# Output products of the recurrent groups, emitted some steps of attention behind the casts of their operands

## The chip, the cores and the metric

The kernel runs on one core of one Trainium2 chip. What is measured is the time of one execution in device microseconds; of several runs the median counts. TensorE is called PE here, its weight loads PEld, VectorE DVE, ScalarE ACT, GpSimd POOL, and the engine that issues the loads from memory SP.

## The reference, cut to what matters

The reference is a trunk of two layers over 256 context tokens and 512 latent tokens of width 1024. In each layer one input projection is split into three groups: A is latent attention with 4 heads, B a bidirectional mLSTM, C a bidirectional RG-LRU. Their outputs are put side by side and go through one output projection.

```python
def token_mixing(ul, uc, ...):
    al, ml_, rl = jnp.split(ul @ w_in, split_at, axis=-1)
    ...
    ya_l, ya_c = mla_mixer(al, ac, rope, g_q, w_uq, g_kv, w_ukv, with_ctx_out)
    yb_l, yb_c = mlstm_mixer(ml_, mc, ml_gate_bias, with_ctx_out)
    yc_l, yc_c = rglru_mixer(rl, rc, conv_w, conv_b, w_a, b_a, w_x, b_x, lam, with_ctx_out)
    y_l = jnp.concatenate([ya_l, yb_l, yc_l], axis=-1) @ w_out
...
        xl = xl + g1l * yl
        xl = xl + g2l * squared_relu_mlp(modulate(rms_norm(xl), sh2l, sc2l), w_ff1[l], w_ff2[l])
```

The last layer needs no output for the context tokens, so there most work is on the 512 latent tokens alone.

## The kernel before, in words

Everything is held transposed: features on the 128 partitions, tokens along the free dimension. A float32 operand is split into a rounded part and a rest (names ending in h and l, or whi and wlo for weights), and a product is three matmuls: h by whi, l by whi, h by wlo. ACT makes the rounded part by a cast, DVE the rest by a subtraction (`split_raw` at lines 165 to 169 for weights, `split_act` at lines 177 and 178 for activations). `dense` (line 196) runs such products over the chunks of the contraction, and yields a cost behind each chunk; one chunk on one range of tokens is called a step here, three matmuls.

The output projection is cut in two. `out_proj` multiplies the half of w_out that belongs to attention once attention is done. `ybc` multiplies the other half, for groups B and C, beside attention: it splits the four chunks of their outputs (tiles yBCh and yBCl), and then, for four pieces of w_out, splits the weights and runs two chunks of output, for each range of tokens four steps into a PSUM tile `outp`, which `gated_add` (line 426, on DVE) adds to x. Layer 0 works on both ranges of tokens (256 and 512 wide, 64 steps in all), layer 1 on the latent one (32 steps).

Two lists of work are written as generators and woven by `weave`: it always advances the one whose sum of yielded costs is the smaller. One is the input projection of attention, its queries and `attention`; the other is mlstm and then `ybc`, whose costs are scaled by PACE["ybc"] (3.0 in layer 0, 3.28 in layer 1). In `attention` a block is 128 queries of one head: `scores` (lines 1035 to 1039 into S, then maximum, exp and scaling into pr), one iteration later `transpose` of pr (line 1057, into pT, split by lines 1062 and 1063), another later `values` for two blocks (line 188 into py); the last block of a head also runs yA. Blocks of layer 0 that belong to the context have 256 keys, all others 768.

The order in which the weave calls things is the order of emission. The framework's planner then puts instructions on the engines: it ranks them by order of emission and takes, in its own model of the time, the first that is ready and has its buffers. `tc.issue_after` keeps the weight splits of `ybc` behind the last cast and the last subtraction of the queries. On the chip each engine runs its list as planned.

Buffers that matter: PSUM pool p1 (2 buffers, shared by outp of `ybc` and py), p2 (3 buffers: S, pT, yA and outp of `out_proj`), 4 raw weight buffers and 3 for each of whi and wlo.

Of the kernel before, what the change touches and what calls it, by code (L numbers as in the profile page):

```python
# [26 lines left out]
NMR = 6  # L27

PACE = {"gates": (1.0, 0.79), "lru": (0.67, 0.86), "mod": (1.76, 0.0), "ml": (1.21, 0.73),
        "tail": (1.5, 1.05), "ybc": (3.0, 3.28), "att": (1.0, 0.91), "dot": (7.2, 0.0), "pause": (55.0, 0.0),  # L30
        "inter": (1.2, 1.2), "scores": (1.02, 1.2), "products": (1.0, 1.0), "outputs": (0.33, 0.39),
        "lru0": (0.75, 1.57), "gates0": (3.9, 3.0), "queries": (0.6, 1.0)}
EPS = 1e-6
# [29 lines left out]
def trunk_kernel(ctx, tc, ins, out, dbg=None):  # L63
# [18 lines left out]
    def slot(tag, name, dt=F32, shape=None):  # L82
        return view(sl.tile([128, T if tag in NARROW else SB // 4], dt, tag=tag, bufs=SLOTS[tag], name=name), shape)
# [12 lines left out]
    def ps1(name="p1"):  # L96
        return pp.tile([128, 512], F32, tag="p1", bufs=2, name=name)
# [63 lines left out]
    def split_raw(src, shape, raw=None):  # L161

        if raw is None:
            raw = wp.tile(shape, F32, tag="raw", bufs=NRAW, name="raw")
            dma(raw, src)
        hi = wp.tile(shape, F32R, tag="whi", name="whi")
        lo = wp.tile(shape, F32R, tag="wlo", name="wlo")
        nc.scalar.copy(hi, raw)  # L168
        V.tensor_tensor(lo, raw, hi.bitcast(F32), op=OP.subtract)  # L169
        return hi, lo  # L170

    def split_act(src, a, b, tag, name, shape=None, tag2=None, after=None):

        hi = slot(tag, name + "h", F32R, shape)
        lo = slot(tag2 or tag, name + "l", F32R, shape)
        h, w = (hi[:, a:b], lo[:, a:b]) if shape is None else (hi, lo)
        i0 = nc.scalar.copy(h, src)
        i1 = V.tensor_tensor(w, src, h.bitcast(F32), op=OP.subtract)
        if after is not None:
            after["last"] = i0, i1  # L180
        return hi, lo
# [8 lines left out]
    def dense(ps, wk, rk, segs, M=128, po=PO):  # L190

        n = len(wk)
        for k in range(n):
            for i, (a, b) in enumerate(PASSES):
                for t0, t1 in segs:
                    mm(ps[:M, po + t0:po + t1], wk[k][a], rk[k][b][:, t0:t1],  # L196
                       start=(k == 0 and i == 0), stop=(k == n - 1 and i == 2))
            yield 1e-3 * (segs[-1][1] - segs[0][0]) * 1.3
# [224 lines left out]
    def gated_add(l, v, m, ps, segs, po=PO):  # L423
        for s in segs:
            r = cond(s)
            V.scalar_tensor_tensor(x[m][:, s[0]:s[1]], ps[:, po + s[0]:po + s[1]],  # L426
                                   modv[l][:, v, m, r:r + 1], x[m][:, s[0]:s[1]],
                                   op0=OP.mult, op1=OP.add)
# [913 lines left out]
    for l in range(L):  # L1342
# [53 lines left out]

        def ybc():
            y = [split_act(t[:, t0:], t0, T, tg, "yBC") for t, tg in zip(z["o"] + z["gb"], "zzzz")]
            for mp in range(NK // 2):
                with tc.issue_after(z["last"][0].ins), tc.issue_after(z["last"][1].ins):  # L1400
                    w = split_raw(ins["w_outc"][l, 1, mp], [128, 2, 4, 128])
                for mi in range(2):
                    for s in segs:
                        ps = ps1("outp")
                        yield from dense(ps, [(w[0][:, mi, j], w[1][:, mi, j]) for j in range(4)], y, [s], po=-s[0])
                        gated_add(l, 2, 2 * mp + mi, ps, [s], po=-s[0])
        run(weave(chain(in_mla(l, u, z, t0), in_outgates(l, u, z, t0), slow(mla_queries(l, z, t0), PACE["queries"][l]),
                        slow(attention(l, z, t0), PACE["att"][l])),
                  chain(slow(mlstm(l, z, t0), PACE["ml"][l]), until(lambda: "yA" in z), slow(ybc(), PACE["ybc"][l]))))
        spans = [s for sw in sweeps for s in sw]  # L1410
        norm = Norm(segs, D, "n2")
# [105 lines left out]
```

## Time and profile before

| | |
|---|---|
| median of 3 runs | 1606.79 us (1605.44 to 1609.7) |
| profiled execution, its own time | 1607.73 us |
| its span, first to last instruction | 1605.9 us |
| mean granted clock of TensorE | 0.987 |
| PE busy | 97% |
| DVE busy | 73% |
| ACT busy | 45% |

The span is the time between the first and the last instruction that the profile shows; the rest of the profiled execution's time lies around it. Busy shares are means over stages with different limits, so the stage of the change has to be looked at by itself. Attention with `ybc` beside it runs from about 272 to 380 us in layer 0 and from about 1128 to 1212 us in layer 1.

### The profile page before, as it was taken

How to read it: one execution, taken by the hardware profiler on the slowest of the kernel's cores; microseconds unless marked ns; L12 is line 12 of the kernel's file. 1: busy time of each engine (PE TensorE's matmuls, PEld its weight loads, DVE VectorE, ACT ScalarE, POOL GpSimd, SP SyncE). 2: the span in 40 equal slices, each digit the busy share in tenths (PEclk: the TensorE clock that was granted, in tenths of full speed). 3: DMA queues.
4: the chain of work that ended last, by engine and by line, in shares of the span. 5: the costliest groups of instructions: out<-in, count | busy, mean ns of one | idle time of the engine just before them, and what ended most of it. 6: DMA issues, size and time to landing. Idle time of an engine off the chain costs nothing.

```text
span 1605.9 us, 24415 instructions
## 1 busy us (share of the span) xinstructions
PE 1550.6 (97%) x9588; PEld 1352.5 (84%) x9588; DVE 1167.1 (73%) x2271; ACT 717.8 (45%) x1194; POOL 63.0 (4%) x104
## 2 busy tenths in 40 slices
PE   8999999999989999999999998999999899999997
PEld 4667897898879899999999986887789789888897
DVE  4795577777785888777577787866878867666667
ACT  4462225444454233334335445623655535444453
POOL 1201010000000000000000001111000000000000
PEclk9999999999999999999999999999999999999999
DMA  9558121102113434335243521312103132232233
GB/s 332 163 201 304 43 60 66 40 14 79 54 40 105 131 106 157 119 119 171 79 146 126 190 80 41 113 53 76 66 27 112 47 102 96 93 106 93 92 109 115
DMA packets 57874, 171.22 MB, mean 107 GB/s; under 512 B 6640, under 2 KB 18672, under 8 KB 57760
## 3 DMA queue, kind: packets, MB, share of 16 engines
q1 hardware_dynamic: 54496, 161.92, 30.3%
q0 software_dynamic: 2112, 6.70, 1.5%
q8 instruction: 75, 1.23, 0.3%
q10 hardware_dynamic: 1152, 1.05, 0.2%
q14 instruction: 39, 0.32, 0.1%
HBM read 166.09 MB, written 2.15 MB: 105 GB/s over the span
## 4 chain that ended last, share of the span: by engine, by line
PE 76%; DVE 6%; issue 3%; ACT 2%; DMA 1%; POOL 0%; POOLq 0%; DVEq 0%; ACTq 0%
PE ff L196 26%; PE str L1211 14%; PE outp L196 6%; PE inp L196 6%; PE strq L1211 5%; PE first L458 3%; PE py L188 2%; PE S L1035 2%; PE kvp L188 2%; PE pT L1057 2%; PE pn L878 1%; DVE usum L1154 1%; PE S L1039 1%; PE S L1037 1%; DVE usum L1159 1%
## 5 line engine op out<-in xcount | busy, mean ns | idle before, releaser
L196 PE MATMUL ff<-hh,whi 128*128 128x512 f32 (+1 forms) x800 | 243.8, 351 | 3.5 <-ACT hrelu L1114 3.3
L196 PE MATMUL ff<-hl,whi 128*128 128x512 f32 (+1 forms) x800 | 244.1, 351 | 0.0
L196 PE MATMUL ff<-hh,wlo 128*128 128x512 f32 (+1 forms) x800 | 243.0, 349 | 0.0
L168 ACT CAST whi<-raw 128x1024 fp32r<-128x1024 f32 x137 | 143.4, 1049 | 214.8 <-PE inp L196 47.5
L169 DVE TENSOR_TENSOR wlo<-raw,whi 128x1024 fp32r<-128x1024 f32 x137 | 167.4, 1222 | 75.4 <-ACT whi L168 73.3
L1191 ACT CAST whi<-raw 128x512 fp32r<-128x512 f32 x156 | 93.4, 619 | 211.9 <-PE ff L196 106.7
L426 DVE SCALAR_TENSOR_TENSOR x<-ff,mod,x 128x256 f32<-128x256 f32 (+1 forms) x200 | 123.5, 638 | 77.8 <-PE ff L196 77.3
L196 PEld LDWEIGHTS ff<-hh,whi 128*128 128x128 f32 x800 | 150.9, 189 | 22.9 <-ACT hrelu L1114 3.9
L196 PEld LDWEIGHTS ff<-hl,whi 128*128 128x128 f32 x800 | 151.2, 189 | 20.9 <-DVE hl L1220 1.6
L196 PEld LDWEIGHTS ff<-hh,wlo 128*128 128x128 f32 x800 | 150.9, 189 | 20.5
L1192 DVE TENSOR_TENSOR wlo<-raw,whi 128x512 fp32r<-128x512 f32 x156 | 104.0, 685 | 28.4 <-ACT whi L1191 27.3
L1211 PE MATMUL str<-t,whi 128*128 128x384 f32 (+1 forms) x520 | 118.9, 316 | 0.6 <-ACT whi L1191 0.6
L305 DVE SCALAR_TENSOR_TENSOR modjunk<-modw,cb 128x512 f32<-128x512 f32 x128 | 87.6, 686 | 7.2 <-DMA modw<-in_w_modT 2.9
L1211 PEld LDWEIGHTS str<-t,whi 128*128 128x128 f32 x520 | 90.0, 190 | 2.7 <-ACT whi L1191 0.9
L1211 PE MATMUL str<-t,wlo 128*128 128x384 f32 (+1 forms) x260 | 82.1, 316 | 0.0
L1211 PE MATMUL str<-uh,whi 128*128 128x256 f32 (+1 forms) x260 | 81.2, 312 | 0.6 <-ACT hrelu L1225 0.6
L1211 PE MATMUL str<-ul,whi 128*128 128x256 f32 (+1 forms) x260 | 79.6, 306 | 0.0
L1211 PE MATMUL str<-uh,wlo 128*128 128x256 f32 (+1 forms) x260 | 79.5, 306 | 0.0
L1211 PE MATMUL strq<-uh,whi 128*128 128x384 f32 (+1 forms) x208 | 65.1, 313 | 8.6 <-ACT whi L1191 8.6
L196 PE MATMUL inp<-uh,whi 128*128 128x256 f32 (+1 forms) x224 | 70.2, 370 | 0.0
L196 PE MATMUL inp<-uh,wlo 128*128 128x256 f32 (+1 forms) x224 | 66.4, 355 | 0.8 <-DVE wlo L169 0.8
L196 PE MATMUL inp<-ul,whi 128*128 128x256 f32 (+1 forms) x224 | 66.8, 356 | 0.0
(369 smaller groups left out, 3699.1 us busy)
## 6 DMA issues: line engine op xcount, KB each, us to landing
raw<-in_w_ff2c SPq DMA_DIRECT2D x72, 512.0 KB, 3.6
raw<-in_w_ff1c SPq DMA_DIRECT2D x64, 512.0 KB, 3.5
modw<-in_w_modT SPq DMA_DIRECT2D x48, 512.0 KB, 3.6
modw<-in_w_mod SPq DMA_DIRECT2D x32, 512.0 KB, 4.7
raw<-in_w_outc SPq DMA_DIRECT2D x24, 512.0 KB, 3.5
raw<-in_w_inc SPq DMA_DIRECT2D x21, 512.0 KB, 3.7
modw<-in_w_mod SPq DMA_DIRECT2D x32, 256.0 KB, 5.4
raw<-in_w_inkv SPq DMA_DIRECT2D x8, 512.0 KB, 3.5
```

The lines of the kernel that those rows point to most:

```text
L168: nc.scalar.copy(hi, raw)
L169: V.tensor_tensor(lo, raw, hi.bitcast(F32), op=OP.subtract)
L188: mm(dst, w[a], r[b], start=first and i == 0, stop=last and i == 2)
L196: mm(ps[:M, po + t0:po + t1], wk[k][a], rk[k][b][:, t0:t1], start=(k == 0 and i == 0), stop=(k == n - 1 and i == 2))
L305: V.scalar_tensor_tensor(junk, w[:, 512 * i:512 * i + 512], 1.0, rows[2 * r + i], op0=OP.mult, op1=OP.mult, accum_out=acc[:, m, i, r:r + 1])
L426: V.scalar_tensor_tensor(x[m][:, s[0]:s[1]], ps[:, po + s[0]:po + s[1]], modv[l][:, v, m, r:r + 1], x[m][:, s[0]:s[1]], op0=OP.mult, op1=O ...
L458: mm(ps[:M, PO + s[0]:PO + s[1]], wk[k][a][:, :M], self.rk[k][b][:, s[0]:s[1]], start=(k == 0 and i == 0), stop=(k == NK - 1 and i == 2))
L1035: mm(S[:, PO + a:PO + e], z["qk"][h][wa][:, qs], ckv[ra][:, a:e], start=(i == 0), stop=False)
L1057: nc.tensor.transpose(pt[:, PO + 128 * k:PO + 128 * k + 128], pr[:, 128 * k:128 * k + 128], ident)
L1191: nc.scalar.copy(hi, src)
L1192: V.tensor_tensor(lo, src, hi.bitcast(F32), op=OP.subtract)
L1211: mm(dst, hl[a][:, k], right[k][name][b], start=first and k == 0 and i == 0, stop=last and k == KH - 1 and i == 2, skip_group_check=True)
```

## The change

`ybc` yields once more, behind the splits of its four operands and ahead of the first split of weights. The yield is 2.5, scaled like its others by 3.0 in layer 0 and 3.28 in layer 1. Everything that `ybc` emits from there on comes that much later beside attention.

```diff
-        "tail": (1.5, 1.05), "ybc": (3.0, 3.28), "att": (1.0, 0.91), "dot": (7.2, 0.0), "pause": (55.0, 0.0),
+        "tail": (1.5, 1.05), "ybc": (3.0, 3.28), "att": (1.0, 0.91), "dot": (7.2, 0.0), "ahead": 2.5, "pause": (55.0, 0.0),
...
         def ybc():
             y = [split_act(t[:, t0:], t0, T, tg, "yBC") for t, tg in zip(z["o"] + z["gb"], "zzzz")]
+            yield PACE["ahead"]
             for mp in range(NK // 2):
                 with tc.issue_after(z["last"][0].ins), tc.issue_after(z["last"][1].ins):
                     w = split_raw(ins["w_outc"][l, 1, mp], [128, 2, 4, 128])
```

## Rows read from the trace of the kernel before

**Rows 1.** The page's first part: busy time, share of the span, instructions.

```profile
PE 1550.6 (97%) x9588; PEld 1352.5 (84%) x9588; DVE 1167.1 (73%) x2271; ACT 717.8 (45%) x1194; POOL 63.0 (4%) x104
```

**Rows 2.** Table by stretch: length, busy PE, PEld, DVE, ACT, POOL; clock, DMA, GB/s.

```profile
290.00:380.00 90.00, 89.86 (x603) 79.82 (x602) 65.42 (x149) 43.76 (x95) 0.00 (x0) 1.00 0.06 19
1138.00:1212.00 74.00, 73.87 (x470) 64.26 (x468) 55.61 (x114) 37.29 (x77) 0.00 (x0) 1.00 0.10 34
1212.00:1227.00 15.00, 15.00 (x127) 14.91 (x126) 13.17 (x23) 8.42 (x15) 0.00 (x0) 1.00 0.45 141
...
273.34:282.17 8.83, 5.91 (x17) 4.32 (x18) 8.80 (x15) 8.80 (x13) 0.00 (x0) 0.67 0.47 143
1131.50:1137.74 6.24, 5.35 (x19) 3.23 (x20) 6.24 (x11) 5.77 (x8) 0.00 (x0) 1.00 0.57 188
```

**Rows 3.** PE's waits, 265 to 382 and 1118 to 1240: total us, times, longest.

```profile
PE outp L196 <- ACT yBCh L177: 2.3, 1, 2.3
PE outp L196 <- DVE oll L1077: 0.5, 1, 0.5
...
PE qrp L196 <- DVE ckvTl L178: 1.4, 1, 1.4
PE outp L196 <- DVE wlo L169: 0.5, 1, 0.5
```

**Rows 4.** Timeline, start of attention in layer 0: start, us, engine, line, work [idle before].

```profile
273.06 0.28 PE L1039 MATMUL S<-krhll,qr 128*128 128x256 f32 x1
...
273.84 1.04 ACT L168 CAST whi<-raw 128x1024 fp32r<-128x1024 f32 x1
...
274.79 0.83 ACT L177 CAST yBCh<-o 128x768 fp32r<-128x768 f32 x1
...
275.67 0.62 PE L196 MATMUL outp<-yBCh,whi 128*128 128x256 f32 x2 [2.33 <-ACT yBCh L177]
...
276.62 1.22 DVE L169 TENSOR_TENSOR wlo<-raw,whi 128x1024 fp32r<-128x1024 f32 x1
...
278.62 0.41 DVE L1042 TENSOR_REDUCE mx<-S 128x1 f32<-128x256 f32 x1
...
282.17 0.63 PE L1057 MATMUL pT<-ident,pr 128*128 128x128 f32 x2
```

**Rows 5.** Timeline, start of attention in layer 1, all engines.

```profile
1130.41 2.00 ACT L168 CAST whi<-raw 128x1024 fp32r<-128x1024 f32 x2
...
1131.51 0.50 PE L196 MATMUL outp<-yBCh,whi 128*128 128x512 f32 x1
...
1131.85 0.51 PE L1039 MATMUL S<-krhll,qr 128*128 128x256 f32 x2
...
1134.14 0.95 DVE L1042 TENSOR_REDUCE mx<-S 128x1 f32<-128x768 f32 x1
...
1135.74 1.04 ACT L168 CAST whi<-raw 128x1024 fp32r<-128x1024 f32 x1
...
1137.74 0.82 PE L1057 MATMUL pT<-ident,pr 128*128 128x128 f32 x6
```

**Rows 6.** Table by half microseconds, PE alone, layer 0: length, busy, clock, DMA.

```profile
276.50:277.00 0.50, 0.32 (x1) 0.50 0.65 115
...
282.50:283.00 0.50, 0.50 (x4) 0.50 0.65 262
...
283.50:284.00 0.50, 0.50 (x5) 1.00 0.94 98
```

**Rows 7.** Timeline: end of ybc's products in layer 0, and in layer 1.

```profile
384.40 0.39 PE L196 MATMUL outp<-yBCh,wlo 128*128 128x512 f32 x1
384.63 0.28 PE L196 MATMUL outp<-yAh,whi 128*128 128x256 f32 x1
...
1213.10 0.74 DVE L426 SCALAR_TENSOR_TENSOR x<-outp,mod,x 128x512 f32<-128x512 f32 x1
```

**Rows 8.** Timeline of SP, 240 to 270: loads of w_outc in layer 0.

```profile
254.07 2.26 SPq L165 DMA_DIRECT2D raw<-in_w_outc  x3
```

## Prediction

> **What bounds the kernel now.** I read the engine rows of the page first: TensorE (PE) is busy for 1550.6 of 1605.9 us, VectorE (DVE) for 73% and ScalarE (ACT) for 45% [rows 1]. So PE idles 1605.9 - 1550.6 = 55.3 us in the whole span, and a change of order, which adds and removes no work, can only move time through that idle, or through stretches in which PE ran at its lower clock. The table by stretch says where the two attention stages stand [rows 2]. Between 290 and 380 us (layer 0) PE is busy for 89.86 of 90.00 us, between 1138 and 1212 us (layer 1) for 73.87 of 74.00 us, and behind it, from 1212 to 1227, for 15.00 of 15.00 us. There is nothing to win in these, and something to lose only if a new wait opens. What is left is the start of each stage. PE's waits [rows 3] name it: in layer 0, 2.3 us for the cast of the first yBCh; in layer 1, 0.5 us for wlo. The timelines show why. In layer 0 PE has finished the scores of the first two blocks by 273.34 (the last one, 273.06 + 0.28) and its next piece of attention, the transpose of the first block's pr, starts at 282.17 [rows 4]. The reader should see what fills the 8.83 us between: 17 output products of the recurrent groups, from 275.67 on, and the ACT and DVE queues, which are both busy for 8.80 of the 8.83 us [rows 2]. Layer 1 has the same picture from 1131.51 to 1137.74: 19 PE instructions [rows 2], the two scores at 1131.85 and 17 output products [rows 5]. The clock rows add a loss that waits don't show: in layer 0 the granted clock is 0.50 (1.2 GHz) from 276.5 to 283.0 and 1.00 (2.4 GHz) from 283.5 on [rows 6]; before it fell PE had been idle for 2.33 us [rows 4].
>
> **What moves.** I walked the yields of the two branches by PACE. ybc's yields are scaled by 3.0 and 3.28, so the new yield of 2.5 is 7.5 units in layer 0 and 8.2 in layer 1. A block's scores cost attention 2.0, its transposes 1.2 and a pair's values 1.9 units (times 0.91 in layer 1, a third of each for blocks with 256 keys). In layer 0, 7.5 units let attention emit scores 1 to 3, transposes 0 to 2 and the first values ahead of the first weight split and product; in layer 1, 8.2 units let scores 1 to 3 and transposes 0 and 1 ahead. The casts stay where they were. All later output products slip by as much, and the rate stays, so more are left when attention has emitted its last step: of 64 steps of three matmuls in layer 0, 14 instead of 9; of 32 in layer 1, 6 instead of 2. No instruction is added.
>
> **Does emission order bind?** It is the first question, since between emission and the engines stands a planner that ranks by order of emission, but issues in its model whatever is ready. The trace says how far it reaches ahead. By the yields the second weight split of layer 1 is emitted 17.5 units behind the casts, behind the transposes of block 4, and the third 35 units behind them, after half of attention. Yet the ACT row at 1130.41 holds the first and second whi together, and the third whi runs at 1135.74, all before the first transpose at 1137.74 [rows 5]. The products do the same: by the yields two steps (six matmuls) precede the first transpose in either layer, and 17 did [rows 2]. So idle engines are filled with work emitted far later, and a delay of 7.5 or 8.2 units, well under those 17.5 and 35, doesn't keep the products out of the hole. That carries the forecast.
>
> **Term 1, the hole in layer 0.** It contains 8.83 - 5.91 = 2.92 us of idle [rows 2]. The 2.33 us in it end when ACT has gone through whi and the cast of yBCh, one behind the other [rows 4]; the casts are not moved, and the product needs whi too, so swapping these two changes nothing. What can change is DVE: wlo (1.22 us at 276.62) loses rank against the maximum of the second block's scores (0.41 us at 278.62) [rows 4]. Upper bound: that op goes ahead and the third pass waits 0.41 us longer. Lower bound: the 2.92 - 2.33 = 0.59 us of small waits go. I take 0, between the ends: more than one product is ready beside the one that waits.
>
> **Term 2, the start in layer 1.** Its idle is 6.24 - 5.35 = 0.89 us [rows 2]. In the same way the bounds are -0.89 and +0.95 us (one maximum over 768 keys ahead of wlo [rows 5]). Again 0.
>
> **Term 3, the slip.** Five steps, 15 matmuls, in layer 0 and four, 12 matmuls, in layer 1 go behind attention. The 512-wide ones start 0.23 us apart [rows 7]; for the 256-wide ones I estimate half, 0.12, and half of layer 0's are such, so that is about 15 x 0.175 = 2.6 us and 12 x 0.23 = 2.8 us that attention ends sooner and the products end later. Both sides are PE work in stretches without idle [rows 2], so the sum is 0. Today the output projection follows the last product of layer 0 with no gap (384.40 to 384.63) [rows 7]; a longer tail of products only covers the last casts of attention better, which already cost nothing. The gated adds go with them: in layer 1 one more (0.74 us [rows 7]) falls into the stretch from 1212 to 1227, where DVE is busy for 13.17 of 15.00 us [rows 2]; bounds 0 and +0.74, and I take 0 since 1.83 us are free there. If that cover is gone, the output projection's split weights are 0.74 us late.
>
> **Term 4, queues and buffers.** Each layer's four loads of w_outc move with the weight splits. SP issued three of layer 0's at 254.07 to 256.33, some 20 us before their use [rows 8], so 7.5 units are covered by the planner's reach; nothing else on SP is queued behind them in the stage, and POOL gets nothing of ybc. The products share two PSUM buffers with the values of attention; this cost one wait of 0.5 us (oll) in layer 0 [rows 3]. I bound it by -0.5 and +0.5 and take 0.
>
> The sum is 0, with term bounds from -0.6 - 0.9 - 0.5 = -2.0 to +0.4 + 0.95 + 0.7 + 0.5 = +2.6 us. The profiled execution took 1607.73 us (span 1605.9 and 1.8 us around it), 0.9 us above the median of the three runs, 1606.79. I predict the median again: **1606.8 us**. A run-to-run spread of 1605.4 to 1609.7 means that about 0.3%, 4.8 us, can be told from no change.
>
> **Rivals.** (1) *Slower: the fill is lost.* If the delayed rank really keeps the products behind attention's next steps, PE stands still from 273.34 until the first transpose, and from about 1132 to 1137.7. The price is the fill at full speed (in layer 0 twelve of the 17 are 256 wide): 12 matmuls x 0.12 + 5 x 0.23 = 2.6 us in layer 0 and 17 x 0.23 = 3.9 us in layer 1, 6.5 us in all; and in layer 1 a hole of about 5 us, longer than the 2.33 us before which the clock fell, would add a dip like the one of layer 0, 6.5 us at half rate [rows 6] or 3.3 us. Together +6.5 to +9.8 us: 1613 to 1617. It decides from the point where fewer than half of the 34 fill matmuls stand ahead of the first transposes. Against it speak the early whi casts [rows 5]. The Trainium skill, page "TensorE: Matmul & The Clock Gate", section "What's actually happening", speaks for the dearer end: it calls the throttled state the default, released by activity, so a longer idle is paid for again in clock. The trace agrees in layer 0 [rows 6]; in layer 1, behind a wait of 1.4 us for ckvTl [rows 3], the hole still has 1.00 [rows 2]. By that rule the rival gives 1617, by waits alone 1613.
>
> (2) *Faster: the start gets short enough for the clock.* With three wlo (1.2 us each) no longer ahead of the softmax of the first blocks on DVE, the first transpose and the scores behind it come up to 2.4 us sooner and PE has no gaps after 275.67. If the dip (3.3 us) then goes too, with the 2.0 us of the bounds above, that is -5.3 us: 1601.5. Against it: the 2.33 us idle ahead of the dip stays, since the casts that end it stay.
>
> (3) *The slip opens waits in the saturated part.* Without products between them for the first blocks, attention's own PE work waits on softmax. It needs DVE or ACT to be the bound there; from 290 to 380 DVE is busy for 65.42 of 90 us [rows 2]. Price: 1 to 4 us, 1608 to 1611.
>
> **How the numbers follow.** Forecast (sum within -2.0 and +2.6): 0.55. Rival 1: 0.17; rival 2: 0.15; rival 3: 0.13. Rival 1 is beyond 4.8 us, nearly all; rival 2 about two thirds; rival 3 hardly. Adding a little for reordering in later stages that I can't follow: faster 0.14, within 0.3% 0.68, slower 0.18. The forecast's own range is 1604.8 to 1609.4; rival 3 and the near parts of 1 and 2 bring it to **1602 to 1613**.
>
> **What would show it.** Right: in the changed kernel some 15 products still stand ahead of the first transposes in each layer, the wait for yBCh is still above 2 us and the dip of the clock is still there; 5 and 4 more steps follow the last yA product, without idle. Wrong on fill: the transposes follow the scores on PE after a wait on ACT or DVE, with whi casts behind them. Wrong on the slip: waits of py, pT or S on DVE or ACT between 290 and 380 us. Wrong on the clock: no stretch at 0.50 near 276 us, or a new one near 1134 us.

## The result, and the profile after

The changed kernel takes 1615.89 us (median of six runs, 1612.63 to 1620.09) against 1606.22 us for the kernel before (six runs, 1605.44 to 1609.7, the three of the first table among them): a ratio of 1.0055, 95% interval 1.0041 to 1.007, which is 6.6 to 11.2 us. The forecast was no change; its range ended at 1613. The profiled execution took 1614.98 us, its span is 1613.2 us (before 1605.9), the mean clock 0.985 (before 0.987).

No work was added. This is the page's first line, as in [rows 1]:

```profile
PE 1552.1 (96%) x9588; PEld 1355.8 (84%) x9588; DVE 1167.9 (72%) x2271; ACT 717.9 (45%) x1194; POOL 63.0 (4%) x104
```

PE's busy time has grown by 1.5 us, so most of the 7.3 us of span is idle time. To find it, measure each attention stage from its first score matmul to the first matmul of the MLP (tile `first`). Layer 0's stretch went from 147.62 to 151.03 us, layer 1's from 108.32 to 113.03: +3.41 and +4.71, together 8.1 us. That is as much as the whole loss, 7.3 us of span in this one execution and 6.6 to 11.2 us of time.

PE's waits from 265 to 382 and from 1118 to 1240 us, columns as in [rows 3]:

```profile
PE pT L1057 <- DVE pr L1047: 8.2, 1, 8.2
PE qrp L196 <- DVE ckvTl L178: 0.5, 1, 0.5
...
PE outp L196 <- DVE wlo L169: 2.2, 1, 2.2
PE qrp L196 <- DVE ckvTl L178: 1.4, 1, 1.4
```

The 2.3 us wait for yBCh in layer 0 has become a wait of 8.2 us of the first transpose; the 0.5 us wait for wlo in layer 1 has become 2.2 us. The table by stretch, columns as in [rows 2]: first the hole of layer 0 and its saturated part, then the start of layer 1, its saturated part and what follows.

```profile
273.56:281.80 8.24, 0.01 (x1) 0.03 (x1) 8.21 (x15) 8.21 (x13) 0.00 (x0) 0.69 0.38 127
290.00:377.00 87.00, 86.91 (x581) 77.50 (x580) 63.54 (x147) 43.11 (x95) 0.00 (x0) 1.00 0.04 13
1134.00:1141.30 7.30, 4.61 (x13) 3.08 (x11) 7.16 (x14) 6.75 (x10) 0.00 (x0) 0.69 0.53 178
1146.00:1217.00 71.00, 70.64 (x446) 61.46 (x446) 52.06 (x107) 34.64 (x72) 0.00 (x0) 1.00 0.07 23
1217.00:1230.00 13.00, 13.00 (x98) 12.41 (x97) 9.19 (x15) 6.66 (x11) 0.00 (x0) 1.00 0.33 107
```

The hole of layer 0 is hardly shorter than it was, 8.24 us instead of 8.83, and it is empty: 0.01 us of PE instead of 5.91. DVE and ACT are as full in it as before (8.21 of 8.24 us), since they still do the casts and the weight splits of products that don't come, and the softmax. The parts that were saturated are saturated still. The timeline of layer 0, columns as in [rows 4], shows the odd thing:

```profile
274.07 1.04 ACT L168 CAST whi<-raw 128x1024 fp32r<-128x1024 f32 x1
...
275.02 0.83 ACT L177 CAST yBCh<-o 128x768 fp32r<-128x768 f32 x1
...
276.84 0.42 DVE L1042 TENSOR_REDUCE mx<-S 128x1 f32<-128x256 f32 x1
277.17 1.22 DVE L169 TENSOR_TENSOR wlo<-raw,whi 128x1024 fp32r<-128x1024 f32 x1
...
281.80 0.66 PE L1057 MATMUL pT<-ident,pr 128*128 128x128 f32 x2 [8.24 <-DVE pr L1047]
...
288.10 0.28 PE L188 MATMUL py<-pTh,ckvTh 128*128 128x256 f32 x1
...
288.81 0.28 PE L196 MATMUL outp<-yBCh,whi 128*128 128x256 f32 x1
```

The first product's operands (whi, yBCh) are there at 275.02 + 0.83 = 275.85 us and PE is idle, yet it runs at 288.81, a few matmuls behind the first py. It waits for neither of these operands nor for the engine. In layer 1 ten products come ahead of the first transpose instead of 17; this is its timeline, to be held against [rows 5]:

```profile
1134.09 0.43 PE L196 MATMUL outp<-yBCh,whi 128*128 128x512 f32 x1
...
1134.91 0.95 DVE L1042 TENSOR_REDUCE mx<-S 128x1 f32<-128x768 f32 x1
...
1136.45 2.35 DVE L169 TENSOR_TENSOR wlo<-raw,whi 128x1024 fp32r<-128x1024 f32 x2
...
1137.72 0.79 PE L196 MATMUL outp<-yBCh,wlo 128*128 128x512 f32 x1 [2.24 <-DVE wlo L169]
...
1141.30 1.05 PE L1057 MATMUL pT<-ident,pr 128*128 128x128 f32 x4
```

The second maximum (0.95 us) now stands ahead of the weight differences on DVE. The clock, by half microseconds as in [rows 6], layer 0 and then layer 1:

```profile
282.00:282.50 0.50, 0.50 (x4) 0.50 0.68 205
...
286.50:287.00 0.50, 0.50 (x3) 0.61 0.13 49
287.00:287.50 0.50, 0.50 (x4) 1.00 0.00 0
...
1136.00:1136.50 0.50, 0.00 (x0) 1.00 0.29 115
...
1137.50:1138.00 0.50, 0.28 (x1) 0.50 0.00 0
...
1144.00:1144.50 0.50, 0.50 (x5) 1.00 1.06 418
```

PE starts the transposes of layer 0 at 1.2 GHz and stays there until about 286.9 us; before, only until about 283. Layer 1, which had no such stretch [rows 2], now has one from 1136.5 to 1144.

**The loss of layer 0 from these rows**: the hole 8.24 - 8.83 = -0.6; the 17 products have to be done later, at full clock 2.6 us (the prediction's price); behind the hole (286.9 - 281.8) / 2 = 2.5 us are lost to the clock, where it was about 0.5, so +2.0; the wait for oll is gone, -0.5. Together +3.5, measured +3.41. The clock's term counts only what lies behind the hole; over the whole stretch PE is busy at 1.2 GHz for less time than before (5.1 instead of 6.3 us), because before most of that time lay inside the hole, whose length is now 0.6 us less.

### The profile page after: what moved, and what is told of

Same layout as the page of the kernel before. It is cut to its first block, busy times and chain, and to the rows that moved or that the text cites. A ratio compares the mean times of both kernels' runs of the same rounds, so it can differ in the third digit from the quotient of the medians.

```text
span 1613.2 us, 24421 instructions
## 1 busy us (share of the span) xinstructions
PE 1552.1 (96%) x9588; PEld 1355.8 (84%) x9588; DVE 1167.9 (72%) x2271; ACT 717.9 (45%) x1194; POOL 63.0 (4%) x104
## 4 chain that ended last, share of the span: by engine, by line
PE 76%; DVE 6%; issue 3%; ACT 2%; DMA 1%; POOL 0%; POOLq 0%; DVEq 0%; ACTq 0%
PE ff L196 26%; PE str L1211 14%; PE outp L196 6%; PE inp L196 6%; PE strq L1211 5%; PE first L458 3%; PE py L188 2%; PE S L1035 2%; PE kvp L188 2%; PE pT L1057 2%; PE pn L878 1%; DVE usum L1154 1%; PE S L1039 1%; PE S L1037 1%; DVE usum L1159 1%
```

## The experiments

The theory that I formed on these rows has two causes. *A, buffers*: a product tile and a tile of attention's values (py) share the two PSUM buffers of pool p1, and the planner gives the buffers out in the order in which the program, as emitted, takes the tiles. A product tile emitted behind the first py can't start before py has its buffer, that is not before the first transposes, however ready its operands are. *B, rank*: the first weight difference (wlo) falls behind the second maximum on DVE. The rivals are the rank of the products themselves on PE, the clock, and the slip as such.

The kernels of the table are taken up one by one below it. All stretches are from one profile each. "Idle" is PE's idle time in the stretch, "half" the time that PE was busy at 1.2 GHz in it, "ahead" how many products (single matmuls) stand ahead of the first transpose (layer 0, layer 1). "Half" is read to about 0.1 us.

| kernel | ahead | layer 0 us | idle | half | layer 1 us | idle | half | ratio to before |
|---|---|---|---|---|---|---|---|---|
| before | 17, 17 | 147.62 | 3.68 | 6.3 | 108.32 | 1.24 | 0 | 1 |
| after | 0, 10 | 151.03 | 8.47 | 5.1 | 113.03 | 3.15 | 5.9 | 1.0055 (1.0041 to 1.007) |
| l0_only | 0, 17 | 151.08 | 8.48 | 5.2 | 108.35 | 1.22 | 0 | 1.0019 (1.0008 to 1.0031) |
| claim | 17, 15 | 149.52 | 5.71 | 6.1 | 111.65 | 3.30 | 3.4 | 1.0041 (1.0029 to 1.0053) |
| claim_one | 10, 10 | 150.32 | 5.15 | 8.4 | 111.89 | 3.16 | 3.3 | 1.0047 (1.0027 to 1.0067) |
| l0_hot | 0, 17 | 150.23 | 5.01 | 3.3 | 108.33 | 1.25 | 0 | 1.0016 (1.0005 to 1.0028) |
| wfirst | 0, 10 | 151.08 | 8.41 | 5.4 | 113.37 | 2.78 | 6.0 | 1.0042 (1.0027 to 1.0057) |
| wclaim | 17, 17 | 148.58 | 4.80 | 6.4 | 110.33 | 2.93 | 0 | 1.0019 (1.0009 to 1.003) |
| fill | 17, 17 | 147.74 | 4.97 | 3.3 | 109.33 | 1.99 | 0 | 1.0009 (0.9996 to 1.0022) |
| pyp2 | 17, 15 | 149.39 | 4.76 | 6.0 | 114.62 | 4.11 | 6.2 | 1.0042 (1.0026 to 1.0058) |
| tilesfirst | 17, 17 | 146.88 | 4.10 | 3.1 | 109.00 | 1.46 | 0 | 1.0003 (0.9993 to 1.0014) |
| prev1 | 17, 17 | 147.02 | 3.13 | 6.5 | 108.84 | 2.05 | 0 | 0.9993 (0.9984 to 1.0002) |
| y3 | 24, 24 | 148.81 | 5.96 | 6.0 | 111.43 | 3.61 | 3.2 | 1.0035 (1.0022 to 1.0049) |
| y3_l0 | 24, 17 | 148.87 | 5.96 | 6.1 | 108.23 | 1.25 | 0 | 1.0005 (0.9995 to 1.0016) |

Two things make the stretches readable. Layer 1 came out at 108.32, 108.35, 108.33 and 108.23 in four kernels whose layer 1 is the same; layer 0 of after and l0_only at 151.03 and 151.08, of y3 and y3_l0 at 148.81 and 148.87. And the two differences to before, added and divided by 1606 us, lie in the interval of the ratio for every kernel: wclaim (0.96 + 2.01) / 1606 = 0.0018, after 8.12 / 1606 = 0.0051. The parts are less sure than the sum. What is left of a stretch when idle time and half of "half" are taken off is 140.8 us in layer 0 of before, and from 139.9 to 141.6 in the others (l0_hot, with its added matmuls, left out); so idle time and clock account for a difference between stretches only to within 1 to 2 us.

**l0_only: the delay in layer 0 alone.**

```diff
-"ahead": 2.5
+"ahead": (2.5, 0)
-            yield PACE["ahead"]
+            yield PACE["ahead"][l]
```

> The new yield stays in layer 0 alone (0 units in layer 1). Measure beside the time: from the first S matmul to the first matmul of the MLP, 147.6 us in layer 0 and 108.3 in layer 1 before the change, 151.0 and 113.0 with it. If each layer's loss is made in that layer: 151.0 and 108.3, the whole 3.4 us above before, +0.2%. If the loss of layer 1 follows from the state that layer 0 leaves: 151.0 and about 113, +0.5%.

Layer 0 has the loss of the change (151.08), layer 1 none (108.35): the two losses are separate.

**claim: the two tiles are taken ahead of the new yield.**

```diff
             y = [split_act(t[:, t0:], t0, T, tg, "yBC") for t, tg in zip(z["o"] + z["gb"], "zzzz")]
+            held = [ps1("outp") for _ in range(2)]
+            for t in held:
+                mm(t[:, 0:1], ident, ones, start=True, stop=True)
             yield PACE["ahead"]
...
-                        ps = ps1("outp")
+                        ps = held.pop(0) if held else ps1("outp")
```

> As the change, but two matmuls of one column each, emitted with the casts, write to the first two PSUM tiles of the products, so that these tiles stand ahead of the first tile of the values (py) in the order in which the shared pool of two buffers is granted; the products themselves stay as late in emission as the change puts them. Theory A (buffer order): the hole is filled again, 15 to 17 products stand ahead of the first transpose in both layers, the stretches go back to about 147.6 and 108.5, time within 0.15% of before. Theory B (rank: products lose to attention's pieces that are ready) or C (the slip and the longer tail cost the time): stretches 151 and 113, +0.5%.

PE's waits in the kernel claim, layer 0 and then layer 1:

```profile
PE outp L196 <- ACT yBCh L177: 2.3, 1, 2.3
PE pT L1057 <- DVE mx L1043: 1.6, 1, 1.6
PE py L188 <- ACT pTh L1062: 0.6, 1, 0.6
...
PE outp L196 <- DVE wlo L169: 2.0, 1, 2.0
```

The products are emitted as late as in the changed kernel, and yet the hole is filled again: the first wait is the 2.3 us for yBCh of [rows 3]. But layer 0 wins back 1.5 of 3.4 us and layer 1 1.4 of 4.7, and layer 1 still waits 2.0 us for wlo. Neither theory's stretches (147.6 and 108.5, or 151 and 113) came out: A is real and is not all.

**claim_one: only the first of the two tiles is taken** (`range(1)` in the edit above).

> The same with one tile in place of two. Theory A: one tile's products can go early, about 10 of 17 in both layers; layer 0 lies between its two values, about 149 us, layer 1 as with the change, about 113; +0.35 to +0.45%. Theories B and C: 151 and 113.

Ten products stand ahead, and both stretches (150.32, 111.89) lie between after and claim. Neither is the one expected (149 and 113). Layer 1 has as many products ahead as after has, the same idle time (3.16 against 3.15 us) and the same wait of 2.2 us for wlo; it is shorter by 1.1 us because PE was busy at 1.2 GHz for 3.3 us instead of 5.9. What set the clock apart isn't shown. The same holds for claim, whose layer 1 has 3.30 us of idle time and 3.4 at half: its 1.4 us are nearly all clock (2.5 us less at half are worth 1.3), and can't be credited to the buffers.

**l0_hot: as l0_only, with 14 matmuls put into the hole, whose result nobody uses.**

```diff
+            if l == 0:
+                hot = ps1("hot")
+                for _ in range(14):
+                    mm(hot, y[0][0][:, t0:t0 + 128], y[0][0][:, t0:t0 + 512], start=True, stop=True)
             yield PACE["ahead"][l]
```

> As the run with the yield in layer 0 alone, with 14 matmuls of 512 columns in layer 0 that multiply the first cast operand with itself into a PSUM tile that nobody reads, emitted behind the casts: PE is busy in the hole with no useful work. If the clock has a share in the loss: the stretch of half clock behind the first transpose (4.8 us of work at half rate) shrinks to that of before, and layer 0 comes to about 149 us, 2 us less than without them. If it is only the lost products: 151.

The hole is now 2.33 us idle, 3.46 us of these matmuls at full clock and 2.44 us idle; 3.4 us behind it run at half clock instead of the 5 us of after. The stretch is 0.85 us shorter than in l0_only, where 2 us were expected. So the clock is a part of layer 0's loss. The other 2.6 us aren't free of it: 3.4 / 2 = 1.7 us are still lost to it behind the hole, where before lost 0.5. By the sum above the rest is the 2.6 us of products that weren't done, less 0.6 of hole and 0.5 of oll.

**wfirst: B alone undone**; the first split stands ahead of the yield, the products behind it.

```diff
+            with tc.issue_after(z["last"][0].ins), tc.issue_after(z["last"][1].ins):
+                w = split_raw(ins["w_outc"][l, 1, 0], [128, 2, 4, 128])
             yield PACE["ahead"]
             for mp in range(NK // 2):
-                with tc.issue_after(z["last"][0].ins), tc.issue_after(z["last"][1].ins):
-                    w = split_raw(ins["w_outc"][l, 1, mp], [128, 2, 4, 128])
+                if mp:
+                    with tc.issue_after(z["last"][0].ins), tc.issue_after(z["last"][1].ins):
+                        w = split_raw(ins["w_outc"][l, 1, mp], [128, 2, 4, 128])
```

> The changed kernel with one part put back: the first weight split of each recurrent group (its cast and its difference) is emitted ahead of the new yield, as in the kernel before; all products stay behind it. By the order of emission the products still have no buffer ahead of the first values of attention in layer 0 (none of 17 ahead of the first transposes) and one of the two in layer 1 (10 of 17). Theory 'buffer order and rank of the difference': only the second of two causes is taken out, so layer 0 keeps its hole of 8.2 us and its stretch from the first scores to the MLP stays at 150.5 to 151.3 us (before 147.6, after 151.0), since no product could use an earlier difference there; layer 1 gains the wait for the difference (2.2 us back to 0.6): 111.0 to 112.0 (before 108.3, after 113.0). Time 1613 to 1615. Rival 'rank alone' (the difference that comes behind the maxima is the whole cause, and the buffers follow from it): both layers return to within 0.7 us of before, 1606 to 1608.

Layer 0 as expected (151.08, "rank alone" is out). Layer 1 missed: 113.37, not 111 to 112. PE's waits in layer 1 of wfirst say why:

```profile
PE outp L196 <- ACT yBCh L177: 0.9, 1, 0.9
PE outp L196 <- DVE wlo L169: 0.7, 1, 0.7
PE outp L196 <- DVE yBCl L178: 0.7, 2, 0.4
```

One wait of 2.2 us has become four that sum to 2.3: my reading, which no run isolates, is that with a single buffer there is one tile of products, in which each matmul waits for its own cast, and no second one to step in. The clock falls as in after (5.9 and 6.0 us busy at half).

**wclaim: A and B undone, the products as late as in the change** (the edits of claim and wfirst together).

> The changed kernel with both suspected causes taken out and the later emission of the products kept: the first weight split stands ahead of the new yield, and the two buffers of the first two product tiles are claimed there by one 128x128x1 matmul each, whose result the first product overwrites (two matmuls a layer are added). By the order of emission 17 products stand ahead of the first transposes in both layers, and the casts, the differences and the maxima stand as in the kernel before. Theory 'buffer order and rank of the difference': the two causes together are the whole loss, so both stretches return to the kernel before's, 147.3 to 148.2 us in layer 0 and 108.0 to 109.0 in layer 1, holes of about 2.3 and 0.6 us, time within 0.15% of before. Rival 'the slip itself costs' (products that come later push work behind the attention or leave the recurrence late, whatever buffers they have): the claimed kernel's 149.5 and 111.6 us stay to more than half, 1611 to 1614.

148.58 and 110.33: of the loss 2.4 of 3.4 us and 2.7 of 4.7 us are gone, but neither theory's number is met. PE's waits that remain in wclaim, layer 0 and layer 1:

```profile
PE outp L196 <- ACT yBCh L177: 2.3, 1, 2.3
PE pT L1057 <- DVE pr L1047: 1.1, 1, 1.1
PE py L188 <- ACT pTh L1062: 0.6, 1, 0.6
...
PE yA L196 <- DVE x L426: 1.3, 1, 1.3
```

The holes are those of before (2.3 us, and no half clock in layer 1). New are waits behind them, inside attention: at 288.5 and 298.7 us, and at 1156.1 us ahead of a yA, where before ran three products (1156.39 to 1157.08) while the cast of ol was under way. PE in wclaim, layer 0 and then layer 1:

```profile
288.51 0.85 PE L1057 MATMUL pT<-ident,pr 128*128 128x128 f32 x6 [1.08 <-DVE pr L1047]
298.67 0.39 PE L188 MATMUL py<-pTh,ckvTh 128*128 128x256 f32 x1 [0.57 <-ACT pTh L1062]
...
1154.34 0.39 PE L196 MATMUL outp<-yBCh,wlo 128*128 128x512 f32 x1
1156.06 0.50 PE L196 MATMUL yA<-olh,wuvh 128*128 128x512 f32 x1 [1.33 <-DVE x L426]
```

So there is a third cause, *C*: delayed products leave idle time between attention's own steps. It is of the kind of rival 3 of the prediction. The trace fits: behind the two claimed tiles no product starts from 287.0 to 298.9 us of layer 0 and none but the one at 1154.34 from 1142.2 to 1161.0 of layer 1; the longest pauses between products there in before are 5.1 and 9.0 us. That the pause alone makes the waits is not shown, for layer 1 of before has 9.0 us without one.

With the four kernels after, wfirst, claim and wclaim the two causes can be set against each other. Undoing B alone gives nothing (151.08, 113.37). Undoing A alone gives 1.5 us in layer 0, and in layer 1 the 1.4 us that are mostly the clock's. Undoing both gives 2.4 and 2.7. C is what is left, 1.0 and 2.0. In layer 1 the 2.7 us are clock as well: the idle time is hardly less than in after (2.93 against 3.15 us), but it has moved from the start into attention, and no half clock follows it.

**fill: the same yield, 1.0 in layer 0 and 0.4 in layer 1.**

```diff
-"ahead": 2.5
+"ahead": (1.0, 0.4)
```

> The changed kernel with a smaller amount of delay: 1.0 in layer 0 and 0.4 in layer 1 instead of 2.5 in both, which are the largest whose two first product tiles are still emitted ahead of the first tile of values (threshold between 1.0 and 1.5 units in layer 0 for the second tile's rank to matter, between 0.4 and 0.7 in layer 1); 17 products stand ahead of the first transposes in both layers. Theory 'buffer order and rank of the difference': the buffers are got in time, the difference stands behind a maximum only in so far as the delay passes one, so layer 0 loses at most 1.9 us (147.6 to 149.5) and layer 1 at most 1.0 (108.3 to 109.3); time 1606 to 1610, and the loss is a step in the delay and not proportional to it. Rival 'loss grows with the delay' (proportional: 3.4 us x 1.0/2.5 and 4.7 us x 0.4/2.5): 149.0 and 109.1; it can be told from the first only where the stretches come out at 147.6 and 108.3, or where the claimed tiles are absent.

147.74 and 109.33. With 40% of the delay layer 0 loses 0.1 us, not 1.4, which looks like a step and not a slope. But this profile has 3.3 us at half clock where before has 6.3, behind the same 2.3 us wait, which is worth 1.5 us, and its idle time is 1.3 us more than before's; with the clock of before it would have come out at about 149.2, next to the rival's 149.0. The ratio, 1.0009 (0.9996 to 1.0022), allows both. So fill shows that 17 products keep their place under a smaller delay, as A says, and does not settle step or slope. Layer 1 loses 1.0 us, with 0.9 us of idle time inside attention (before 0.2), 0.6 of it in one wait at 1205.8 us: C again, at another place.

**pyp2: the change as it is, but py from the other pool.**

```diff
-            py = ps1("py")
+            py = ps2("py")
```

> The changed kernel, delay and all, with one thing else: the values of attention (py) take their tile from the pool of three two-bank buffers (that of the scores, the transposes and yA) instead of the pool of two single ones that the products use. Theory 'buffer order': with py no longer ahead of them in the pool, 17 products of layer 0 and 15 of layer 1 stand ahead of the first transposes although they are emitted as late as in the changed kernel; the 8.2 us piece of idle time in layer 0 becomes 2.3 to 4.5 us (the weight difference still ranks behind the maxima), layer 0 at 149 to 150 us and layer 1 at 111 to 112.5 as with the claimed tiles, and a further 0 to 1.5 us a layer may be lost where four kinds of tile share three buffers. Rival 'emission order acts on PE's queue directly, and not by the pool': the products stay behind the first values, the 8.2 us hole stays and layer 0 is at 151 us or more.

Not one product is emitted earlier than in the changed kernel, and PE's waits in layer 0 of pyp2 are:

```profile
PE outp L196 <- ACT yBCh L177: 2.3, 1, 2.3
PE outp L196 <- DVE wlo L169: 0.5, 1, 0.5
```

The wait of 8.2 us is gone; the products run in the hole again. With claim this settles A: what kept them out was the buffer that py shared, not their rank on PE. The number of products ahead of the first py says the same in every trace (a tile is twelve matmuls): 0 and 12 in layers 0 and 1 of after and wfirst (0 too in layer 0 of l0_only and l0_hot), 12 and 12 in claim_one, 19 to 24 wherever two tiles come ahead of py, never more than 24. In pyp2, where py stands in the other pool, it is 37 in layer 0 and 21 in layer 1.

Layer 0 meets the expectation (149.39). Layer 1, 114.62, is worse than expected and worse than after. It keeps the 2.0 us wait for wlo, with 6.2 us at half clock, and has 1.9 us of idle time later. The latter could be four kinds of tile in three buffers, but it stands at the end, behind the last product:

```profile
1219.05 0.39 PE L196 MATMUL outp<-yBCh,wlo 128*128 128x512 f32 x1
...
1222.08 0.38 PE L188 MATMUL py<-pTl,ckvTh 128*128 128x256 f32 x1 [0.97 <-DVE pTl L1063]
...
1223.77 0.50 PE L196 MATMUL yA<-olh,wuvh 128*128 128x512 f32 x1 [0.46 <-ACT olh L1076]
```

In before and after seven and thirteen products are left behind the last py of layer 1, here none: freed from py, they ran so early that the end of attention has no fill.

**tilesfirst: the yield moved behind the first weight pair**, so that three quarters of the products slip and the tiles of the first pair (four in layer 0, two in layer 1) don't.

```diff
-            yield PACE["ahead"]
             for mp in range(NK // 2):
+                if mp == 1:
+                    yield PACE["ahead"]
                 with tc.issue_after(z["last"][0].ins), tc.issue_after(z["last"][1].ins):
```

> The changed kernel with the new yield moved behind the first weight pair: the first split and the first four groups of products (two tiles of the latents' columns and two of the context's in layer 0) are emitted as in the kernel before, and the other three quarters of the products are delayed by the same 2.5 units. By the order 17 products stand ahead of the first transposes in both layers. Theory 'what is lost is the fill ahead of the first transposes': stretches 147.4 to 148.0 and 108.1 to 108.8 us, holes of 2.3 and 0.6 us, time within 0.1% of before. Rival 'a third cause, later products fill less of the first steps of attention' (the 1.0 and 2.0 us that stayed with both tiles claimed and the split in its place): 148.3 to 148.8 and 109.5 to 110.5 us, with the idle time inside the attention and not ahead of it.

146.88 and 109.00, sum -0.1 us; ratio 1.0003 (0.9993 to 1.0014), against 1.0055 for the change. So the loss of the change, but for what the interval leaves (2 us at most), hangs on the first weight pair and its products. Where it keeps its place, C nearly vanishes too (idle time inside attention, without the 0.5 us for oll that before has too, 0.5 and 0.4 us, before 0.3 and 0.2). That layer 0 is shorter than before is the clock: 3.1 instead of 6.3 us busy at half, worth 1.6 us, with the same 2.3 us wait ahead of it. With the clock of before it would be about 148.5, 0.9 us longer than before, so a rest of C in layer 0 can't be ruled out.

**prev1: the opposite move on the kernel before**, the first split allowed behind the second latent's cast.

```diff
-                with tc.issue_after(z["last"][0].ins), tc.issue_after(z["last"][1].ins):
+                i0, i1 = z["lasts"][1 if mp == 0 else 3]
+                with tc.issue_after(i0.ins), tc.issue_after(i1.ins):
```

(`z["lasts"]` collects every pair of z["last"].)

> The kernel before, and not the changed one, with the opposite move: the first weight split of each recurrent group is allowed behind the cast of the second latent column instead of the last one, so that its cast and its difference run in idle time of ACT and DVE ahead of the attention. Theory 'the stretch is set by how soon products fill the hole ahead of the first transposes': the first product starts 0.5 to 1.0 us sooner, the hole of layer 0 (2.3 us idle in one piece) falls to 1.3 to 1.8 us, layer 1's 0.6 us wait for the difference goes; layer 0's stretch 146.0 to 147.2 (the lower where the granted clock does not fall behind the hole), layer 1's 107.6 to 108.3; time 1603.5 to 1606.5. Rival 'the hole of the kernel before is set by the first casts of the operands, which this does not touch': both stretches unchanged within 0.2 us, time the same within 0.1%. Rival 'the cast steals ACT or DVE from the latents': the first scores come 0.5 to 1 us later, slower by as much.

The first wait of layer 0 falls from 2.3 to 1.5 us, and 0.6 us of the stretch are won; the clock falls as before. Layer 1 loses 0.5 (108.84, expected 107.6 to 108.3). No measurable change in time.

**y3 and y3_l0: casts, first split and products allowed from the third latent on**, in both layers and in layer 0 alone.

```diff
-    until(lambda: "yA" in z), slow(ybc(), PACE["ybc"][l])
+    until(lambda: len(z.get("lasts", ())) >= 3), slow(ybc(), PACE["ybc"][l])
```

(The condition is shortened; in y3_l0 it holds for layer 0 alone. The first split is allowed as in prev1, in the same layers.)

> The kernel before with the opposite move in both layers: the casts of the products' operands, their first weight split and the products are allowed from the third latent column on instead of from the start of attention, the first split behind the second latent's cast. Some of the casts then run in the 2.3 us of idle time that ACT has ahead of the first scores, and 23 instead of 17 products stand ahead of the first transposes by the order. Theory 'the fill of the hole decides': layer 0's piece of 2.3 us idle falls under 1 us, its 6.8 us at half clock shorten to 3.4 or vanish, stretch 143 to 146.5 (the full gain being 2.3 us of idle time and 3.2 of clock); layer 1, which has 1.0 us of idle time there and no half clock, gains 0 to 0.7: 107.6 to 108.5. Time 1600 to 1606. Rival 'the casts delay the scores instead': the first scores come as much later as the hole is shorter, or the fourth latent's cast waits, so that what the stretches gain the time ahead of them loses; time 1606 to 1609.

> The kernel before with that opposite move in layer 0 alone; layer 1 as before (108.3 us). Theory 'the fill of the hole decides': layer 0 at 143 to 146.5 us, time 1601 to 1606. Rival 'the casts delay the scores': layer 0 starts its scores 0.5 to 2 us later and the time is 1606 to 1608.

Both miss: 148.81 and 148.87 us in layer 0, and 111.43 in layer 1 of y3, where a transpose waits 2.6 us. The casts didn't delay the scores in y3_l0: its first one starts at 271.40 us, before at 271.98. The timeline of y3_l0:

```profile
277.72 0.40 PE L197 MATMUL outp<-yBCh,wlo 128*128 128x512 f32 x1
...
278.85 0.48 DVE L427 SCALAR_TENSOR_TENSOR x<-outp,mod,x 128x256 f32<-128x256 f32 x1
279.31 0.75 DVE L427 SCALAR_TENSOR_TENSOR x<-outp,mod,x 128x512 f32<-128x512 f32 x1
...
282.79 0.66 PE L1058 MATMUL pT<-ident,pr 128*128 128x128 f32 x2 [4.67 <-DVE mx L1047]
```

The products now begin at 271.28 and the 24th, the last of two tiles, ends at 278.12. DVE frees both tiles by 280.06, but no third product tile follows: the next buffer is py's. PE idles for 4.67 us, at the other end of the hole. Until 280.06 both tiles are still held, and behind that the order of the buffers keeps the third tile out. The same two buffers cap the fill: 24 matmuls, whenever they start.

None of these versions is faster than the kernel before by more than the measurement can tell.

## Why the prediction was wrong, point by point

**What bounds the kernel now**: right. The loss is in the two starts that it named and not in the saturated parts.

**What moves**: right in the order (the first py is emitted ahead of the first product in layer 0, the transposes 0 and 1 in layer 1), and the answer was in it: "the first values ahead of the first weight split and product" is the sentence that costs 3.4 us.

**Does emission order bind?** This is the step that failed: "a delay of 7.5 or 8.2 units [...] doesn't keep the products out of the hole". It did, for all 17 in layer 0 and 7 of 17 in layer 1. The prediction saw whi casts of the second and third piece run far ahead of their emission and concluded that products do the same. Weight splits write whi and wlo buffers, which attention's steps don't use, so they reach ahead freely, in the changed kernel too (three of four whi still run ahead of the first transpose of layer 0). Products take p1, and there the order of emission is the order of service. The 17 products of before did run ahead of their emission, but within two tiles that had been taken ahead of the first py: 24 matmuls at most.

**Term 1**: the hole came out at 8.24 us, the fill at 0 instead of 17; the bounds of -0.6 and +0.4 us were bounds on a hole that is still filled.

**Term 2**: the mechanism was seen (a maximum of 0.95 us ahead of wlo) and its size mistaken. The wait grew from 0.5 to 2.2 us, +1.7, and the clock fell behind it: in after 5.9 us busy at half, 3.0 us lost. The bound took the duration of one operation; on DVE, which was full there (7.16 of 7.30 us), the weight difference that lost its place came behind the maximum (0.95 us) and behind the difference of a cast too (0.68 us).

**Term 3**: right that it costs nothing. Products follow attention to the end without idle time, and 1217 to 1230 us is full. The slip itself is smaller than the 15 and 12 matmuls of the sum: behind the last yA stand 34 instead of 25 in layer 0 and 10 instead of 3 in layer 1, 9 and 7 more.

**Term 4**: the term that was mis-sized. It named the two shared buffers and bounded them by the one wait that they show in the trace of before, 0.5 us for oll [rows 3]. That is the price of the buffers in an order that suits them; the other order costs the whole fill, 2.6 us of layer 0's 3.4 by the sum above.

**The rivals**: rival 1 came true, with its point of decision (fewer than 17 of 34 products ahead: it was 10) and its time (1613 to 1617; measured 1615.9), by another mechanism than "rank". In layer 0 the price of the fill, 2.6 us, came within 0.8 us of the 3.4, since the clock behind the hole (+2.0 us), which it left out, was partly made up by the shorter hole and the wait for oll (-1.1). In layer 1 it priced 3.9 + 3.3 us where 4.7 were lost, since one tile still came first. It got 0.17 on the strength of the whi rows, which don't bear on it. For the dearer end the prediction cited the Trainium skill, page "TensorE: Matmul & The Clock Gate", section "What's actually happening", by which throttling is the default and activity lifts it. The trace agrees: layer 1 has a new stretch at 1.2 GHz between 1136.5 and 1144 us, behind the 2.24 us wait, and the time lies between the two ends. Rival 2 didn't occur: the wait for yBCh wasn't shortened. Rival 3 doesn't show in the changed kernel, whose stretch from 290 to 377 us is full; waits of its kind appear as C once the fill is restored, at 1.0 + 2.0 us within its price of 1 to 4.

**What would show it**: "wrong on fill: the transposes follow the scores on PE after a wait on ACT or DVE, with whi casts behind them" came as written, except that the whi casts run ahead. That exception is the sign of a buffer, not of a rank: operands ready, engine idle, instruction late. "Or a new one near 1134 us" came true for the clock of layer 1.

Still open is what sets the place of C: its waits stand elsewhere in each order, and no run took one away by itself. Whether the loss grows in steps or with the delay is open too. And so is why the clock stays low for 6.8 us in some profiles and 3.4 in others behind the same 2.3 us wait (before and wclaim against tilesfirst and fill). Each kernel has one profile here, so 1.6 us of a layer 0 stretch may be chance, though layers of the same order came out alike.

## What to carry to other kernels

Before you let work be emitted later, list every pool that its outputs share with what it is moved past: where buffers are few, order of emission is order of service, and ready operands on an idle engine don't help. Evidence that some instruction reaches ahead holds only for instructions that take the same buffers. And an early filler is worth as much as it fits the hole: two tiles are 24 matmuls, too late they miss the hole, too early they are used up ahead of it.

## What the runs showed of the hardware

The granted clock fell also where no single wait was long: layer 1 of wfirst, with waits of 0.9, 0.7, 0.4 and 0.3 us, went to 1.2 GHz as after did behind 2.2 us, while layer 1 of before, with 0.5 and 0.3, stayed at 2.4. In layer 0 of before and after, idle time of 2.3 us and of 8.2 us cost about the same clock: 6.3 and 5.1 us of work were done at half rate, because half of the longer stretch at 1.2 GHz (10.2 us) lay over the idle time itself. Behind the same 2.3 us, tilesfirst and fill did only 3.1 and 3.3 us of work at half rate.
